# Query norms by transposes and accumulating squares early in a group, in place of products with ones at its end

## The chip, the cores and the metric

The kernel runs on one core of a Trainium2 chip. A core has a matrix engine (TensorE, PE in the profile; PEld is its loading of weights), a vector engine (VectorE, DVE), an engine for activations (ScalarE, ACT), GpSimd (POOL), and queues for transfers, here issued by SyncE (SP). The engines run side by side, each works through its own queue in order, and they wait for each other by semaphores. The metric is the device time of one execution in microseconds. Before the change the median of three runs is 860.6 us (859.97 to 862.24).

## What is computed

One decoder layer on 256 tokens of width 2048: a gated DeltaNet branch and a cross-attention into 256 memory tokens read one input projection; their outputs are gated and go through one output projection. The change touches the end of the DeltaNet branch, where queries are normed and outputs are normed:

```python
q = l2_norm(q) * DN_HEAD_DIM ** -0.5       # per token and head
...
o = gated_delta_rule(q, k, v, g, beta)     # linear in q, in chunks
o = rms_norm(o, out_g)
...
y = jnp.concatenate([mix, xa], axis=-1) * jax.nn.silu(z)
x = x + jnp.einsum("bse,ed->bsd", y, w_out[i])
```

The output is linear in q, so the kernel doesn't norm q: it folds the sum of squares of a query into the epsilon of the output's norm (eq in the code), and needs that sum per token only when the output o of a head is scaled.

## The kernel before

**Tiling and stream.** All weights (273 loads of 128x1024) come one after the other in the order of the list PLAN; I count them from 0. For each load SP starts a transfer into a tile st (five buffers), ACT casts it to the high part of wt (L335, four buffers), DVE subtracts to get the low part (L339), and PE runs 12 or 16 matmuls with high and low parts into pa (keys and queries) or pb (values, gates z, output projection). In the output projection the moving operands are yhi and ylo.

**Side work.** Everything else is generators that PE's stream passes now and then (`step_side`): they give a plan of the time for each engine, and emit their instructions between two matmuls of the stream. `pe_soon` makes a generator wait until PE may take its next block, `until` and `bank` wait for a condition or a free bank of PSUM (tags "m" and "A" have two, "B" one). All of this happens while the program is built. After 45 us of the plan the instructions are put in order by the framework, so that the final order on each engine differs somewhat from the order of the code, and a change of one step moves others. On the chip the order of each engine is fixed.

**A group.** `delta(g)` works on group g of six: two pairs of query and key heads, four value heads. In turn: products pkq of keys and queries (km, kch, kcl); products pU with the inverse Y of the first chunk (u0s, u0, uh, ul); products across the chunks and the first block of pO; products with the second half of Y (u1) and across again (oq); then ACT squares the queries `KQ[p][:, 1]` of both pairs into q2, and PE runs the second pO block and four products pqs of q2 with a column of ones, which give the sums of squares per token. DVE then computes o[1] = pO + oq and eq from pqs; ACT squares o with accumulation (ojunk); DVE computes e = (mean square + eq); POOL raises it to -1/2 (the function `rsqrt`, e<-e,mhalf); DVE scales o by e and by the gates zs, eight times 128x128 a group.

**The outputs.** `split_y` takes the finished outputs by twos of pairs, transposes them on PE (eight transposes into pyT), and writes yhi (ACT) and ylo (DVE). GATHER_Y is the time that it is willing to wait until another generator wants PE, so that their blocks go together. The output projection holds at the first weight whose ylo isn't there.

**The convolution of values** (vc, of vs and taps vw) and of queries and keys (raw, acc) is also DVE work between the loads; inT and inXT belong to the inverse's substitution, pm to its products on PE.

Of the kernel before, what the change touches and what calls it, by code (L numbers as in the profile page):

```python
# [10 lines left out]
AF = mybir.ActivationFunctionType  # L11
ALU = mybir.AluOpType
# [9 lines left out]
NB = 2  # L22
C = 128
EPS = 1e-6
# [9 lines left out]
LOOK = 2  # L34
WARM = 8
GATHER = 0.5
GATHER_Y = 4.0
XPACE = 3.0
HOP = 0.25
PINNED = 45.0  # L40
# [32 lines left out]
def hybrid_kernel(ctx: ExitStack, tc: tile.TileContext, x, xT, memT, W, prm_d, cst_d, out):  # L73
# [32 lines left out]
    def width(ap):  # L106
        n = 1
        for d in ap.shape[1:]:
            n *= d
        return n  # L110
# [14 lines left out]
    ve, se = Engine(nc.vector, ve_cost), Engine(nc.scalar, se_cost)  # L125
# [19 lines left out]
    def S2(name, shape, dt=F32):  # L145
        return s2p.tile([128] + list(shape), dt, name=name, tag="s2")

    def SM(name, shape, bufs=3, dt=F32):
        n = 1
        for d in shape:  # L150
            n *= d
        if n > 128:
            return smp.tile([128] + list(shape), dt, name=name, tag="s1k", bufs=6)
        if n > 16:
            return smp.tile([128] + list(shape), dt, name=name, tag="s512", bufs=3)
        return smp.tile([128] + list(shape), dt, name=name, tag=name, bufs=bufs)

    PB = {"pa": 3, "m": 2, "A": 2, "B": 1}

# [4 lines left out]
    def PS(tag, name):  # L164
        idle[tag].remove(min(idle[tag]))
        pt = ps.tile([128, 512], F32, name=name, tag=tag, bufs=PB[tag])
        held[id(pt)] = (tag, pt)
        return pt

    def spare(tag, n=1):  # L170
        return sum(t <= now[0] for t in idle[tag]) >= n

    def give(pt, t):

        idle[held.pop(id(pt))[0]].append(t)

    def bank(tag, name):
        yield from until(lambda: spare(tag))
        return PS(tag, name)

    def banks(name):
        yield from until(lambda: spare("m", 2))
        return [PS("m", name) for _ in range(2)]
# [10 lines left out]
    def mm(o_, lhsT, rhs, start, stop):  # L194
        n = width(rhs)
        if rhs.dtype == F32:
            now[0] += {32: 0.015, 64: 0.038}.get(rhs.shape[0], max(0.19, 4 * n / 2400.0))
        else:
            now[0] += max(0.092, n / 2400.0 + 0.0137) + 0.01 * (n == 256)
        te.matmul(o_, lhsT, rhs, start=start, stop=stop)  # L200

    def tr(o_, i_):
        now[0] += 0.093
        te.transpose(o_, i_, ident)
# [25 lines left out]
    def until(cond):  # L230
        while not cond():
            yield POLL

    def pe_soon(gather=0.0):

        yield max(fin[0] - now[0], 0.0) + SLACK
        yield "pe", gather
# [9 lines left out]
    def calm(queued=CALM):  # L247

        while ve.end > now[0] + queued:
            yield ve.end - now[0] - queued  # L250
# [5 lines left out]
    ones = cst[:, K_ONE : K_ONE + 1]  # L256
# [606 lines left out]
    KQ = [None] * NPAIR  # L863
# [242 lines left out]
    def split_y():  # L1106
        for j0 in (12, 14, 0, 2, 4, 6, 8, 10):
            jj = (j0, j0 + 1)
            yield from until(lambda: all(yf[j] is not None for j in jj))
            yield from calm(0.8)  # L1110
            yield "pe", GATHER_Y
            pts = yield from banks("pyT")
# [45 lines left out]
    def v_done(g):  # L1158
# [13 lines left out]
        def done(r, pt):  # L1172
            def go():
# [41 lines left out]
                if r == 1:  # L1215
                    vss[g] = raw
                    yield from delta(g)
# [8 lines left out]
    def delta(g):  # L1226

        pp = (2 * g, 2 * g + 1)
# [24 lines left out]
            ve.tensor_tensor(out=kcl[:, i], in0=pkv[i][:, 0:4:2, :], in1=kch[:, i], op=ALU.subtract)  # L1253
            give(pks[i], ve.end)
        yield from pe_soon(GATHER)
        A = yield from bank("A", "pU")
        for w, i, h in heads:
            mm(A[:, w * C : (w + 1) * C], Y[pp[i]][:, 0, h, :], vs[0][:, w, :], start=True, stop=True)
        yield 0.2
        u0s, u0 = S2("u0s", [4, C]), S2("u0", [4, C])  # L1260
        ve.tensor_tensor(out=u0s, in0=A.rearrange("j (h e) -> j h e", h=4),
                         in1=ekd[:, h4].unsqueeze(2).to_broadcast([128, 4, C]), op=ALU.mult)
        se.copy(u0.rearrange("j h e -> j (h e)"), A)
        give(A, max(ve.end, se.end))
        yield
        uh, ul = S2("uh", [4 * C], F32R), S2("ul", [4 * C], F32R)
        u0f = u0s.rearrange("j h e -> j (h e)")
        se.copy(uh, u0f)
        for i, p in enumerate(pp):
            ve.tensor_tensor(out=aT[i], in0=km[:, i].unsqueeze(2).to_broadcast([128, NB, 2, C]), in1=dT[p], op=ALU.mult)  # L1270
        yield
        ve.tensor_tensor(out=ul, in0=u0f, in1=uh, op=ALU.subtract)
        yield from pe_soon(GATHER)
        yield from until(lambda: spare("A") and spare("B"))
        A, B = PS("A", "pU"), PS("B", "pO")
# [19 lines left out]
        A, B = PS("A", "pU"), PS("A", "pO")  # L1295
# [8 lines left out]
        for w in range(4):  # L1304
            se.activation(oq[:, w, :], B[:, w * C : (w + 1) * C], AF.Copy, scale=egc[:, 4 * g + w : 4 * g + w + 1])
        give(B, se.end)
        q2 = S2("q2", [2, 256])
        for i, p in enumerate(pp):
            se.activation(q2[:, i, :], KQ[p][:, 1, :], AF.Square)
        yield from pe_soon(GATHER)  # L1310
        yield from until(lambda: spare("B") and spare("m"))
        B, pq = PS("B", "pO"), PS("m", "pqs")
        for w, i, h in heads:
            mm(B[:, w * C : (w + 1) * C], aT[i][:, 1, h, :], u1[:, w, :], start=True, stop=True)
        for b in range(NB):
            for i in range(2):
                mm(pq[:, 2 * b + i : 2 * b + i + 1], q2[:, i, b * C : (b + 1) * C], ones, start=True, stop=True)
        yield 0.2
        ve.tensor_tensor(out=o[1], in0=B.rearrange("c (h e) -> c h e", h=4), in1=oq, op=ALU.add)
        give(B, ve.end)  # L1320

        eq, e4 = SM("eq", [4], 2), SM("e4", [3, NB, 4], 2)
        ve.tensor_scalar(out=eq, in0=pq[:, 0:4], scalar1=EPS, scalar2=EPS * 128, op0=ALU.add, op1=ALU.mult)
        give(pq, ve.end)
        ready.add(f"d{g}")
        yield
        for b in range(NB):
            for w in range(4):
                junk = SM("ojunk", [C])
# [161 lines left out]
```

## Time and profile before

| | before |
|---|---|
| median of 3 runs | 860.6 us |
| profiled execution | 861.81 us, its span 860.0 us |
| granted clock of TensorE | 1.0 |
| POOL busy | 46.5 us (5%) |
| e<-e,mhalf on POOL | 6 times, 1.64 to 6.49 us |
| pqs on PE | 48 records (each program product is two) |
| pyT of outputs o on PE | 48 records (one for each transpose) |

The page gives the busy time of each engine and, in the chain of waits, what released what on the way to the last instruction. Rows of the timeline read: start in us, length in us, engine, line, operation, written tile <- read tiles, shape, how many, and in brackets how long the engine stood idle before and what ended that. PE's records overlap, so the cost of a matmul is read from start to start, not from its length.

### The profile page before, as it was taken

The numbers are of one execution on the slowest core, as the hardware profiler recorded it, in microseconds if no ns is written. First come the engines' busy times: TensorE is split into PE (matmuls) and PEld (weight loads), VectorE is DVE, ScalarE is ACT, GpSimd is POOL, SyncE is SP. The second block draws the span as 40 slices with busy tenths as digits, with TensorE's granted clock in tenths as the row PEclk, the third lists the DMA queues.
The fourth block names the chain that finished last, engine by engine and source line by source line (L and its number), as shares of the span: only waits on it lengthen the run. The fifth ranks groups of instructions, "written<-read, shape, count | busy, mean of one in ns | idle before, by whom it ended". The sixth has DMA issues, their size and how long they took to land.

```text
span 860.0 us, 13169 instructions
## 1 busy us (share of the span) xinstructions
PE 851.7 (99%) x4789; PEld 711.4 (83%) x4789; DVE 619.3 (72%) x1080; ACT 538.7 (63%) x927; POOL 46.5 (5%) x45
## 2 busy tenths in 40 slices
PE   8999999999999999999999999999999999999998
PEld 5888888888888888888888888787888888888886
DVE  7778896658679974788889999568886665444442
ACT  7655654797744665895976666679875654333331
POOL 1000000000000000001100301100010000000000
PEclk9999999999999999999999999999999999999999
DMA  9865566448677886769867779676754547666650
GB/s 352 307 203 177 170 182 168 152 134 259 206 218 228 261 233 206 253 200 266 241 229 232 217 229 269 204 219 228 239 158 161 177 145 255 231 204 207 201 196 24
DMA packets 145289, 181.59 MB, mean 211 GB/s; under 512 B 24808, under 2 KB 115808, under 8 KB 145224
## 3 DMA queue, kind: packets, MB, share of 16 engines
q1 hardware_dynamic: 144792, 180.47, 66.4%
q8 instruction: 37, 0.61, 0.3%
q10 hardware_dynamic: 432, 0.28, 0.1%
q14 instruction: 28, 0.23, 0.1%
HBM read 167.58 MB, written 6.89 MB: 203 GB/s over the span
## 4 chain that ended last, share of the span: by engine, by line
PE 89%; DVE 3%; ACT 3%; DMA 2%; issue 1%; SPq 0%; ACTq 0%; DVEq 0%
PE pb L86 69%; PE pa L86 11%; PE pO L86 2%; PE pU L86 2%; DMA vc<-vs 1%; DVE wt L339 1%; PE pm L86 1%; DVE vc L103 1%; PE pkq L86 1%; PE pyT L86 1%; ACT dec L103 1%; DMA mst<-memT_d 1%; PE pqs L86 1%; DVE acc L103 1%; PE pkk L86 1%
## 5 line engine op out<-in xcount | busy, mean ns | idle before, releaser
L339 DVE TENSOR_TENSOR wt<-st,wt 128x1024 fp32r<-128x1024 f32 (+1 forms) x274 | 332.3, 1216 | 168.4 <-ACT wt L335 161.4
L335 ACT CAST wt<-st 128x1024 fp32r<-128x1024 f32 (+1 forms) x274 | 286.2, 1048 | 232.9 <-PE pb L86 191.9
L86 PE MATMUL pb<-wt,hkt 128*128 128x512 f32 x1536 | 362.3, 393 | 1.5 <-DVE wt L339 1.5
L86 PEld LDWEIGHTS pb<-wt,hkt 128*128 128x128 f32 x1536 | 284.6, 188 | 60.7 <-DVE wt L339 2.5
L86 PE MATMUL pb<-wt,yhi 128*128 128x512 f32 x512 | 158.2, 390 | 0.0
L86 PE MATMUL pa<-hkt,wt 128*128 128x512 f32 (+1 forms) x768 | 142.7, 341 | 0.4 <-DVE wt L339 0.3
L86 PEld LDWEIGHTS pa<-hkt,wt 128*128 128x128 f32 x768 | 117.8, 188 | 18.2 <-DVE wt L339 1.0
L86 PEld LDWEIGHTS pb<-wt,yhi 128*128 128x128 f32 x512 | 95.8, 188 | 19.6
L86 PE MATMUL pb<-wt,ylo 128*128 128x512 f32 x256 | 99.7, 389 | 0.0
L86 PE MATMUL pb<-wt,mkt 128*128 128x512 f32 x384 | 92.4, 401 | 1.2 <-DVE mkt L103 0.7
L86 PEld LDWEIGHTS pb<-wt,mkt 128*128 128x128 f32 x384 | 73.6, 193 | 18.9 <-ACT wt L335 1.6
L86 PEld LDWEIGHTS pb<-wt,ylo 128*128 128x128 f32 x256 | 48.1, 188 | 10.1
L103 ACT ACT_TABLE_LOAD x31 | 39.8, 1283 | 1.4 <-DVE acc L103 1.0
L103 DVE SCALAR_TENSOR_TENSOR acc<-raw,prm,acc 128x255 f32<-128x255 f32 (+2 forms) x72 | 34.2, 476 | 3.5 <-ACT acc L103 3.2
L103 DVE TENSOR_TENSOR inT<-inXT,inN 96x1 f32<-96x1 f32 (+22 forms) x92 | 29.2, 343 | 2.5 <-DMA inN<-dN 1.7
L103 DVE TENSOR_REDUCE inXT<-inT 96x1 f32<-96x1 f32 (+22 forms) x92 | 28.6, 338 | 0.7
L103 POOL TENSOR_TENSOR e<-e,mhalf 128x8 f32<-128x8 f32 x6 | 20.8, 3474 | 120.3 <-DVE e L103 120.3
L103 DVE TENSOR_TENSOR vc<-vc 128x512 f32<-128x512 f32 x36 | 24.5, 684 | 0.1
L103 POOL TENSOR_TENSOR srk<-skt,mhalf 128x4 f32<-128x4 f32 x6 | 7.1, 1176 | 224.7 <-DVE skt L103 224.7
L103 DVE SCALAR_TENSOR_TENSOR o<-o,e,zs 128x128 f32<-128x128 f32 x48 | 14.0, 344 | 7.0 <-POOL e L103 7.0
L103 DVE TENSOR_TENSOR vc<-vc,vw 128x512 f32<-128x512 f32 x24 | 16.4, 685 | 3.4 <-DMA vc<-vs 2.7
L103 ACT ACTIVATE ojunk<-o 128x128 f32<-128x128 f32 x48 | 14.4, 301 | 5.7 <-DVE o L103 3.7
(202 smaller groups left out, 692.9 us busy)
## 6 DMA issues: line engine op xcount, KB each, us to landing
st<-W_d SPq DMA_DIRECT2D x272, 512.0 KB
erow<-dgc SPq DMA_DIRECT2D x24, 256.0 KB
vw<-dtap SPq DMA_DIRECT2D x24, 256.0 KB
dN<-dec SPq DMA_DIRECT2D x12, 256.0 KB
n<-dN SPq DMA_DIRECT2D x12, 256.0 KB
vc<-vs SPq DMA_DIRECT2D x12, 224.0 KB
vc<-vc SPq DMA_DIRECT2D x12, 224.0 KB
xraw<-xT_d SPq DMA_DIRECT2D x8, 256.0 KB
```

Source lines behind the costliest of these rows:

```text
L86: return lambda *a, **k: pin(getattr(self.eng, op)(*a, **k))
L103: return pin(getattr(self.eng, op)(*a, **k))
L335: pin(se.eng.copy(hi[:, w] if parts > 1 else hi, st[:, w] if parts > 1 else src))
L339: pin(ve.eng.tensor_tensor(out=lo[:, w] if parts > 1 else lo, in0=st[:, w] if parts > 1 else src, in1=hi[:, w] if parts > 1 else hi, op=AL ...
```

## The change

GATHER_Y goes from 4.0 to 0.5. The sums of squares of the queries are computed earlier in the group and by other engines: behind the pU products PE transposes the four 128x128 blocks of queries (query and chunk of tokens) into a bank pqT, and ACT squares each with accumulation along the row, which gives q2, one column for each of the four blocks. The two squares of 128x256 and the four products with ones go. The wait for a bank "m" moves with them, from the step with the second pO to that with pU.

```diff
-GATHER_Y = 4.0
+GATHER_Y = 0.5
...
         yield from pe_soon(GATHER)
-        A = yield from bank("A", "pU")
+        yield from until(lambda: spare("A") and spare("m"))
+        A, pq = PS("A", "pU"), PS("m", "pqT")
         for w, i, h in heads:
             mm(A[:, w * C : (w + 1) * C], Y[pp[i]][:, 0, h, :], vs[0][:, w, :], start=True, stop=True)
+        for w in range(4):
+
+            tr(pq[:, w * C : (w + 1) * C], KQ[pp[w % 2]][:, 1, w // 2 * C : (w // 2 + 1) * C])
...
         se.copy(uh, u0f)
+        q2 = SM("q2", [4], 2)
+        for w in range(4):
+            junk = SM("ojunk", [C])
+            se.activation(junk, pq[:, w * C : (w + 1) * C], AF.Square, accum_out=q2[:, w : w + 1])
+        give(pq, se.end)
...
-        q2 = S2("q2", [2, 256])
-        for i, p in enumerate(pp):
-            se.activation(q2[:, i, :], KQ[p][:, 1, :], AF.Square)
         yield from pe_soon(GATHER)
-        yield from until(lambda: spare("B") and spare("m"))
-        B, pq = PS("B", "pO"), PS("m", "pqs")
+        yield from until(lambda: spare("B"))
+        B = PS("B", "pO")
         for w, i, h in heads:
             mm(B[:, w * C : (w + 1) * C], aT[i][:, 1, h, :], u1[:, w, :], start=True, stop=True)
-        for b in range(NB):
-            for i in range(2):
-                mm(pq[:, 2 * b + i : 2 * b + i + 1], q2[:, i, b * C : (b + 1) * C], ones, start=True, stop=True)
...
-        ve.tensor_scalar(out=eq, in0=pq[:, 0:4], scalar1=EPS, scalar2=EPS * 128, op0=ALU.add, op1=ALU.mult)
-        give(pq, ve.end)
+        ve.tensor_scalar(out=eq, in0=q2, scalar1=EPS, scalar2=EPS * 128, op0=ALU.add, op1=ALU.mult)
```

Since the framework puts the instructions in order, others move too. Three places matter below.

**Group 0, DVE, around load 134 (gates z).** Before, from o = pO + oq on; the two rows of wt are loads 134 and 135:

```order
L103 TENSOR_TENSOR o<-pO,oq 128x512
L103 TENSOR_TENSOR raw<-raw 128x256 [waits Activation_49]
L339 TENSOR_TENSOR wt<-st,wt 128x1024 [waits DMAHW0_49,PE_49]
L103 SCALAR_TENSOR_TENSOR acc<-raw,prm,acc 128x255 [waits Activation_49]
L103 SCALAR_TENSOR_TENSOR e_4173<-e_4173,eq 128x8 [waits Activation_49]
L339 TENSOR_TENSOR wt<-st,wt 128x1024 [waits DMAHW3_49,PE_49]
L103 SCALAR_TENSOR_TENSOR acc<-raw,prm,acc 128x254 [waits DVE_49]
L103 TENSOR_TENSOR vc<-vc 128x512 [waits DMAHW7_49,DMAHW6_49,DMAHW0_49]
L103 SCALAR_TENSOR_TENSOR acc<-raw,prm,acc 128x253 [waits DVE_49]
L103 TENSOR_TENSOR vc<-vc 128x512 [waits DMAHW2_49,DMAHW1_49,Pool_49]
L103 SCALAR_TENSOR_TENSOR o<-o,e_4173,zs 128x128 [waits Pool_49]
```

Now, from behind load 133 on; the row of wt at the end is load 134:

```order
L103 TENSOR_TENSOR vc<-vc 128x512 [waits DMAHW2_49,DMAHW1_49,DMAHW0_49]
L103 TENSOR_TENSOR raw<-raw 128x256 [waits Activation_49]
L103 TENSOR_TENSOR inT<-inXT,inN 96x1 [waits DMAHW6_49,DMAHW3_49,Pool_49]
L103 COPY inN<-inXT 96x16x16 [waits Pool_49]
L103 TENSOR_TENSOR vc<-vc 128x512 [waits DMAHW7_49,DMAHW6_49,DVE_49]
L103 SCALAR_TENSOR_TENSOR e_4167<-e_4167,eq 128x8 [waits Activation_49]
L103 TENSOR_REDUCE inXT<-inT 96x1 [waits DVE_49]
L103 SCALAR_TENSOR_TENSOR o<-o,e_4167,zs 128x128 [waits Pool_49]
L103 SCALAR_TENSOR_TENSOR acc<-raw,prm,acc 128x255 [waits Activation_49]
L103 SCALAR_TENSOR_TENSOR o<-o,e_4167,zs 128x128
L103 SCALAR_TENSOR_TENSOR acc<-raw,prm,acc 128x254 [waits DVE_49]
L339 TENSOR_TENSOR wt<-st,wt 128x1024 [waits DMAHW5_49,Activation_49]
```

Load 134 stood ahead of e; now it stands behind e, behind the wait for POOL, and behind two of the scalings of o. Three loads ahead of these rows the whole convolution of a value tile (twelve steps on vc, raw and acc) has moved from behind load 131 to ahead of it.

**Group 2, loads 175 and 176 (values).** DVE before, from load 175 to load 176:

```order
L339 TENSOR_TENSOR wt<-st,wt 128x1024 [waits DMAHW0_49,Activation_49]
L103 TENSOR_TENSOR vc<-vs,vw 128x512
L103 TENSOR_TENSOR vc<-vc,vw 128x512
L103 TENSOR_TENSOR vc<-vc 128x512 [waits DVE_49]
L103 TENSOR_TENSOR vc<-vc 128x512 [waits DMAHW4_49,DMAHW5_49,DVE_49,Pool_49]
L339 TENSOR_TENSOR wt<-st,wt 128x1024 [waits DMAHW6_49,PE_49,Activation_49]
```

DVE now, from the third step behind load 175 to load 176:

```order
L103 TENSOR_TENSOR vc<-vc 128x512 [waits DMAHW1_49,DMAHW2_49,DMAHW0_49,DVE_49]
L103 TENSOR_TENSOR vc<-vc 128x512 [waits DVE_49]
L103 TENSOR_TENSOR o<-pO,oq 128x512 [waits PE_49,Activation_49]
L103 TENSOR_TENSOR vc<-vc 128x512 [waits DMAHW6_49,DMAHW7_49,DVE_49,Pool_49]
L103 SCALAR_TENSOR_TENSOR e_5562<-e_5562,eq 128x8 [waits Activation_49]
L103 SCALAR_TENSOR_TENSOR o<-o,e_5562,zs 128x128 [waits DMAHW3_49,Pool_49]
L103 SCALAR_TENSOR_TENSOR o<-o,e_5562,zs 128x128
L103 SCALAR_TENSOR_TENSOR o<-o,e_5562,zs 128x128 [waits DVE_49]
L339 TENSOR_TENSOR wt<-st,wt 128x1024 [waits DMAHW5_49,Activation_49]
```

On PE the last matmuls of load 175 and what follows them, before:

```order
L86 MATMUL pb_5498<-wt,hkt 128x512 x3
L86 MATMUL pb_5472<-wt,hkt 128x512 x3
L86 MATMUL pb_5498<-wt,hkt 128x512 x3
L86 MATMUL pm<-Am,XN 32x32 [waits DMAHW6_49,Activation_49]
L86 MATMUL pm<-Am,XN 32x32 [waits DMAHW0_49]
```

and now:

```order
L86 MATMUL pb_5439<-wt,hkt 128x512 x3
L86 MATMUL pb_5455<-wt,hkt 128x512 x3
L86 MATMUL pO<-u_5498,aT 128x128 [waits PE_49,Activation_49]
L86 MATMUL pO<-u_5498,aT 128x128 x3
L86 MATMUL pm<-Am,XN 32x32 [waits DMAHW6_49,Activation_49]
```

The second pO block of group 2 has moved to between load 175 and the inverse's block on Am; before it stood eight loads earlier. On DVE the sum o, e, and three scalings, which wait for POOL, have come in ahead of load 176. On ACT the cast of load 176 now stands behind the four squares of that o.

**Group 3, DVE, between loads 185 and 187 (values).** Before, from load 186 to load 187:

```order
L339 TENSOR_TENSOR wt<-st,wt 128x1024 [waits DMAHW2_49,PE_49]
L103 SCALAR_TENSOR_TENSOR acc<-raw,prm,acc 128x255 [waits Activation_49]
L103 TENSOR_TENSOR u0s<-pU,ekd 128x512 [waits PE_49]
L103 SCALAR_TENSOR_TENSOR acc<-raw,prm,acc 128x254 [waits DVE_49]
L103 TENSOR_TENSOR vc<-vc 128x512 [waits DMAHW5_49,DMAHW4_49,Pool_49]
L103 SCALAR_TENSOR_TENSOR acc<-raw,prm,acc 128x253 [waits DVE_49]
L103 TENSOR_TENSOR vc<-vs,vw 128x512
L103 TENSOR_TENSOR vc<-vc,vw 128x512
L103 TENSOR_TENSOR aT<-km,dec 128x512
L103 TENSOR_TENSOR vc<-vc 128x512 [waits DVE_49]
L103 TENSOR_TENSOR aT<-km,dec 128x512
L339 TENSOR_TENSOR wt<-st,wt 128x1024 [waits DMAHW3_49,Activation_49]
```

Now, the eleven steps from raw on, ahead of load 186:

```order
L103 TENSOR_TENSOR raw<-raw 128x256 [waits Activation_49]
L103 TENSOR_TENSOR vc<-vc 128x512 [waits DVE_49]
L103 SCALAR_TENSOR_TENSOR acc<-raw,prm,acc 128x255 [waits Activation_49]
L103 TENSOR_TENSOR vc<-vc 128x512 [waits DMAHW3_49,DMAHW4_49,DVE_49,Pool_49]
L103 SCALAR_TENSOR_TENSOR acc<-raw,prm,acc 128x254 [waits DVE_49]
L103 SCALAR_TENSOR_TENSOR acc<-raw,prm,acc 128x253 [waits DVE_49]
L103 TENSOR_TENSOR vc<-vs,vw 128x512
L103 TENSOR_TENSOR vc<-vc,vw 128x512 [waits DMAHW7_49,DMAHW6_49,DMAHW0_49]
L103 TENSOR_TENSOR km<-pkq,cst 128x256 [waits PE_49]
L103 TENSOR_TENSOR vc<-vc 128x512 [waits DVE_49]
L103 TENSOR_TENSOR km<-pkq,cst 128x256 [waits PE_49]
L339 TENSOR_TENSOR wt<-st,wt 128x1024 [waits DMAHW2_49,Activation_49]
```

Before, ten steps of the group and of the convolution stood between two weights. Now pkq and pU of this group come later, the steps on u0s and aT stand between other loads, and the most crowded stretch is this one ahead of load 186, with a vc step ahead of its first row.

At the end of the program the last outputs' transposes, which stood on PE ahead of load 222's first matmul, now stand behind its ninth.

## The prediction

> **What bounds the kernel now.** First the page: busy times, then the chain of waits.
>
> ```profile
> span 860.0 us, 13169 instructions
> ...
> PE 851.7 (99%) x4789; PEld 711.4 (83%) x4789; DVE 619.3 (72%) x1080; ACT 538.7 (63%) x927; POOL 46.5 (5%) x45
> ...
> PE 89%; DVE 3%; ACT 3%; DMA 2%; issue 1%; SPq 0%; ACTq 0%; DVEq 0%
> ```
>
> PE is busy for 99% of the span and carries 89% of the chain. So an edit pays only in two ways: it takes instructions out of PE's row of matmuls, or it changes how often PE stands still. The view of PE's waits prices the second (total, times, longest):
>
> ```profile
> PE pb L86 <- DVE wt L339: 2.0, 4, 1.1
> ```
>
> Once it runs, PE waits for nothing but weights whose low part DVE has not yet written, 2.0 us in four waits. Two of the four fall at 580.96 and 594.09 in PE's timeline (start, length, count):
>
> ```profile
> 411.60 9.79 PE L86 MATMUL pb<-wt,hkt 128*128 128x512 f32 x42
> ...
> 577.64 2.88 PE L86 MATMUL pb<-wt,hkt 128*128 128x512 f32 x12
> 580.96 0.73 PE L86 MATMUL pb<-wt,hkt 128*128 128x512 f32 x2 [0.44 <-DVE wt L339]
> ...
> 590.83 2.20 PE L86 MATMUL pb<-wt,hkt 128*128 128x512 f32 x9
> 594.09 3.52 PE L86 MATMUL pb<-wt,hkt 128*128 128x512 f32 x14 [1.06 <-DVE wt L339]
> ```
>
> The first row gives the pace: 42 matmuls, the last 0.39 us long, so (9.79-0.39)/41 = 0.229 us from start to start. By it 580.96 is 0.6 us late (577.64 + 12 x 0.229 = 580.39) and 594.09 is 1.2 us late: 1.8 us together.
>
> **PE's work.** The end of group 5 shows what a product with ones and a transpose cost between two weight matmuls:
>
> ```profile
> 695.84 0.39 PE L86 MATMUL pb<-wt,ylo 128*128 128x512 f32 x1
> 696.07 1.05 PE L86 MATMUL pO<-u,aT 128*128 128x128 f32 x8
> 696.96 0.95 PE L86 MATMUL pqs<-cst,q 128*128 128x1 f32 x8
> 697.77 0.72 PE L86 MATMUL pb<-wt,yhi 128*128 128x512 f32 x2
> ...
> 701.77 0.39 PE L86 MATMUL pb<-wt,ylo 128*128 128x512 f32 x1
> 702.00 1.03 PE L86 MATMUL pyT<-cst,o 128*128 128x128 f32 x8
> 702.79 0.71 PE L86 MATMUL pb<-wt,yhi 128*128 128x512 f32 x2
> ```
>
> The 16 records of pO and pqs add 697.77-695.84-0.229 = 1.70 us, 0.106 each; a group's four products are eight records and take 0.85 us. The eight transposes add 702.79-701.77-0.229 = 0.79 us, 0.099 each, so four new ones take 0.40 us. Saved: 0.45 us a group, **2.7 us** for six. I take the transposes of KQ at the price of pyT, since shape and type are the same. At their recorded length (about 0.27 us, were they not overlapped) four would cost 1.1 us; that end is a rival below.
>
> GATHER_Y only lets the outputs' transposes go sooner and less often together with other blocks. In the rows above pO with pqs in one block and pyT in a block of its own cost the same per record (0.106 and 0.099): I take nothing for it.
>
> **ACT.** Two squares of 256 columns go, four accumulating ones come:
>
> ```profile
> 409.71 0.74 ACT L103 ACTIVATE q<-kq 128x256 f32<-128x256 f32 x2
> ...
> 697.95 0.31 ACT L103 ACTIVATE ojunk<-o 128x128 f32<-128x128 f32 x1 [1.98 <-DVE o L103]
> 698.16 0.19 ACT L103 ACTIVATION_READ_ACCUMULATOR ojunk<-o 128x1 f32 x1
> 698.25 0.29 ACT L103 ACTIVATE ojunk<-o 128x128 f32<-128x128 f32 x1
> ```
>
> One square and its read take 698.25-697.95 = 0.30 us, so 1.2 us come for 0.74: +0.5 us a group on an engine that is 63% busy. They now stand behind the copy uh, and behind them wait casts of weights and later copies of the group. The group of casts on the page shows the cover:
>
> ```profile
> L335 ACT CAST wt<-st 128x1024 fp32r<-128x1024 f32 (+1 forms) x274 | 286.2, 1048 | 232.9 <-PE pb L86 191.9
> ```
>
> ACT idles 232.9 us ahead of casts, 191.9 of them until PE gives a buffer back: casts start as soon as a buffer is free, which is long before PE needs it filled. Were that cover gone, 1.2 us a group would be late where it matters, 7 us at most; I take nothing. The same row prices what moves on SP's queue (around group 0 the shifts of values are issued a load earlier, ahead of the weights of load 132): casts wait for PE, not for the transfers, so a load that lands a microsecond later is hidden, and I take nothing there either.
>
> The wait for a bank of "m" moves from the step with pO to the step with pU. It is a condition while the program is built, and no instruction waits longer for it as such; what it does is push pU back in the order, in group 3 from load 183 to load 185. What follows from that is priced in the groups below.
>
> **What the order moves, group 0.** New on DVE is that the low part of load 134 stands behind e, POOL's power and two scalings. The rows of before that price it, group 5's tail first (DVE and POOL):
>
> ```profile
> 697.16 0.69 DVE L103 TENSOR_TENSOR o<-pO,oq 128x512 f32<-128x512 f32 x1
> ...
> 699.26 0.17 DVE L103 SCALAR_TENSOR_TENSOR e<-e,eq 128x8 f32<-128x8 f32 x1 [1.15 <-ACT ojunk L103]
> 701.24 0.88 DVE L103 SCALAR_TENSOR_TENSOR o<-o,e,zs 128x128 f32<-128x128 f32 x3 [1.82 <-POOL e L103]
> 702.04 1.22 DVE L339 TENSOR_TENSOR wt<-st,wt 128x1024 fp32r<-128x1024 f32 x1
> ...
> 699.57 1.64 POOL L103 TENSOR_TENSOR e<-e,mhalf 128x8 f32<-128x8 f32 x1 [41.52 <-DVE e L103]
> ```
>
> ```profile
> 416.64 0.42 DVE L103 TENSOR_TENSOR raw<-raw 128x256 f32<-128x256 f32 x1 [0.49 <-ACT raw L103]
> ...
> 420.03 0.48 DVE L103 SCALAR_TENSOR_TENSOR acc<-raw,prm,acc 128x254 f32<-128x254 f32 x1
> 420.43 0.69 DVE L103 TENSOR_TENSOR vc<-vc 128x512 f32<-128x512 f32 x1
> 421.03 0.48 DVE L103 SCALAR_TENSOR_TENSOR acc<-raw,prm,acc 128x253 f32<-128x253 f32 x1
> ```
>
> raw waited for ACT until 416.64, and I leave it there. Behind it now come two small steps on inT and inN and a vc ahead of e: 0.6 for the vc (421.03-420.43), at most 0.42 for raw, and 0.3 each for the small ones, an estimate near raw's. That is 1.6 us, so e starts at 418.2. From e to the first scaling group 5 took 701.24-699.26 = 1.98 us; two scalings (0.3 each) and two acc (0.40, from 420.03 to 420.43) make 1.4; the low part takes 1.22. Load 134 is ready at 422.8. PE wants it 38 matmuls after 411.60, at 420.3, and 0.45 us earlier by the work saved. PE stands for 422.8-419.9 = **2.9 us**. Below: if raw comes 0.7 us sooner, 2.2. Above: if the value convolution, now ahead of load 131, starts no earlier than before, everything is some 1.2 us later, and POOL may be slow: 5.0.
>
> **Group 2.** The second pO block now stands right behind load 175's matmuls, and load 176 is behind the whole tail on DVE (o, e, POOL, three scalings) and its cast behind the four squares of o on ACT. It is group 5's tail word for word: the low part started 702.04-696.07 = 5.97 us after pO, ready at 7.2. PE meanwhile has pO (0.89, from 696.07 to 696.96) and the inverse's block:
>
> ```profile
> 552.72 0.26 PE L86 MATMUL pm<-Am,XN 32*32 32x32 f32 x8
> ...
> 554.69 1.19 PE L86 MATMUL pb<-wt,hkt 128*128 128x512 f32 x4
> ...
> 552.43 1.23 DVE L339 TENSOR_TENSOR wt<-st,wt 128x1024 fp32r<-128x1024 f32 x1 [3.94 <-ACT wt L335]
> ```
>
> That block takes 1.97 us and a start of 0.1; before, load 176 was ready (552.43 + 1.23) a microsecond ahead of its use at 554.69. Now PE wants it 3.0 us after pO begins: it stands for 7.2-3.0 = **4.2 us**. Nothing below 3.5 follows from these rows unless group 2's pO comes earlier than its place in the order; the upper end is POOL's:
>
> ```profile
> 534.67 4.83 POOL L103 TENSOR_TENSOR e<-e,mhalf 128x8 f32<-128x8 f32 x1 [13.13 <-DVE e L103]
> ...
> 535.58 0.68 DVE L103 TENSOR_TENSOR vc<-vs,vw 128x512 f32<-128x512 f32 x1
> ...
> 419.06 2.56 POOL L103 TENSOR_TENSOR e<-e,mhalf 128x8 f32<-128x8 f32 x1 [11.76 <-DVE e L103]
> ```
>
> The same eight columns took 4.83 and 2.56 us while DVE worked on vc, and 1.64 where DVE stood still (699.57). At both new places DVE stands still behind the power, so I take 1.64; with the longer ones 3.2 and 0.9 us are added.
> [...]
>
> **Group 3.** The two waits at 580.96 and 594.09 go: the blocks of six and ten steps ahead of loads 183 and 187 are broken up, and the most crowded gap now lies ahead of load 186 (twelve steps; with 0.6 for a vc and 0.4 for the others 6.0 us). With two low parts of 1.22 that makes 8.4 us from the cast of load 185; a buffer is four loads old, 4 x 12 x 0.229 = 11 us, when PE comes to it, and km, pU and the new transposes lengthen that. Load 186 still lands some 2 to 3 us early. **-1.8 us**; if a like wait forms there, nothing.
>
> **The end.** The last outputs' transposes move back by nine matmuls, to three before their first use. In before (PE, ACT):
>
> ```profile
> 716.50 1.03 PE L86 MATMUL pyT<-cst,o 128*128 128x128 f32 x8
> ...
> 717.65 1.26 ACT L103 ACTIVATE yhi<-pyT,prm 128x512 fp32r<-128x512 f32 x2
> ```
>
> From their start to the first yhi are 1.15 + 0.63 = 1.8 us; PE has 0.79 of them and 3 x 0.229 = 0.7: **+0.3 us**, between 0 and 0.6.
>
> **Sum.** -2.7 + 2.9 + 4.2 - 1.8 + 0.3 = +2.9 us: a span of 862.9, and with 1.8 us around it 864.7 for an execution like the profiled one (861.8). That one lies 1.2 us above the median of the three runs, 860.6, so I forecast **863.4**. A measurement here can tell about 0.3% from no change, 2.6 us: below 858.0 or above 863.2.
>
> **Rivals.**
> - Neither wait forms (0.12): DVE reaches the weights earlier than I think. Only work, group 3 and the end count: 856.4. For it: of all waits in before none is behind POOL's power. Against: the order puts the weights there.
> - One of the two forms (0.20): 859.2 with group 0's alone, 860.6 with group 2's.
> - POOL's power is long at both places (0.08), as in 534.67: 863.4 + 3.2 + 0.9 = 867.5, slower. It decides from about 1.6 us on.
> - PE falls back to half pace after standing 4.2 us (0.04). At the start it ran so:
>
> ```profile
> 1.21 3.59 PE L86 MATMUL warm<-warm 128*128 128x512 bf16 x8 [1.21 <-DVE warm L103]
> 8.67 4.63 PE L86 MATMUL pb<-wt,mkt 128*128 128x512 f32 x10 [0.27 <-DVE wt L339]
> ```
>
>   0.46 us a matmul for 4.6 us after the last pause, against 0.229 later: ten matmuls, 2.3 us, 865.7. Against: no pause in before is longer than 1.2 us once it runs, so no row shows a fall.
>   [...]
> - The transposes don't overlap (0.04): six groups pay 1.1 for 0.85 us, +1.5 in place of -2.7, 867.6. The pyT rows speak against it.
>
> **Chances.** My forecast has 0.52; spread by 1.3 us either way it lies a little more often above 863.2 than below, 0.28 to 0.24. With the rivals: slower 0.44, same 0.44 (one wait alone falls here), faster 0.12. The range leaves out the case without waits and the far ends of the slow ones: 858.4 to 866.8.
>
> **What would show it.** Right: PE with 4765 records; two waits of pb for wt of about 3 and 4 us, at some 420 and 555, each ending with a wt that follows o scalings after POOL's e; none at 580 and 592; POOL's e near 1.6 us there. Wrong: PE's wait for wt under 3 us in all, or a wait at places not named.

## The result, and the profile after

The changed kernel takes 869.3 us (867.9 to 871.4, four runs) beside 861.4 us before: the ratio is 1.0096, its 95% interval 1.0078 to 1.0114. It is slower, as forecast, but by some 8 us where 2.9 were worked out, and 869.3 lies above the range's end of 866.8. The profiled execution took 867.9 us against 861.8, so 6.1 us of the loss can be looked up in it. The page of the kernel after:

```profile
span 866.1 us, 13173 instructions
...
PE 852.8 (98%) x4765; PEld 711.3 (82%) x4765; DVE 619.6 (72%) x1080; ACT 541.1 (62%) x963; POOL 40.3 (5%) x45
...
PE 85%; issue 8%; ACT 2%; DMA 2%; DVE 1%; POOL 1%; ACTq 0%; SPq 0%; DVEq 0%; POOLq 0%
```

PE has 24 records less, as expected (4765), and is yet busy 1.1 us longer. Work that went but left PE busier means that some of its matmuls took longer. PE's waits in the kernel after:

```profile
PE pb L86 <- DVE wt L339: 3.2, 4, 2.4
PE pO L86 <- ACT u L103: 2.6, 1, 2.6
...
PE pm L86 <- issue: 1.0, 1, 1.0
```

There is one long wait for a weight, not two, and a new one for ACT's copy u. The long wait for a weight is group 2's. In the timeline after (PE, then DVE and POOL):

```profile
553.13 1.05 PE L86 MATMUL pO<-u,aT 128*128 128x128 f32 x8
557.28 0.73 PE L86 MATMUL pb<-wt,hkt 128*128 128x512 f32 x2 [0.26 <-ACT wt L335]
560.38 0.80 PE L86 MATMUL pb<-wt,hkt 128*128 128x512 f32 x1 [2.36 <-DVE wt L339]
...
565.84 2.93 PE L86 MATMUL pb<-wt,hkt 128*128 128x512 f32 x6
568.56 1.73 PE L86 MATMUL pa<-hkt,wt 128*128 128x512 f32 x7
...
554.29 0.69 DVE L103 TENSOR_TENSOR o<-pO,oq 128x512 f32<-128x512 f32 x1 [8.00 <-PE pO L86]
...
558.31 0.87 DVE L103 SCALAR_TENSOR_TENSOR o<-o,e,zs 128x128 f32<-128x128 f32 x3 [1.82 <-POOL e L103]
559.11 1.22 DVE L339 TENSOR_TENSOR wt<-st,wt 128x1024 fp32r<-128x1024 f32 x1
...
556.64 1.64 POOL L103 TENSOR_TENSOR e<-e,mhalf 128x8 f32<-128x8 f32 x1 [18.53 <-DVE e L103]
```

From pO to the low part of load 176 are 559.11-553.13 = 5.98 us; 5.97 was forecast. PE's waits there are 1.0 (in the inverse's block, for its own issue), 0.3 and 2.4 us. But behind the wait six matmuls take 2.93 us, about 0.46 from start to start ((2.93-0.63)/5, the last being 0.63 long) where 0.229 is the pace. The view by windows shows why (window, busy time of PE, PEld, DVE, ACT, POOL, granted clock, share of DMA, GB/s):

```profile
552.00:556.00 4.00, 3.01 (x81) 2.57 (x81) 1.29 (x2) 1.77 (x9) 0.00 (x0) 1.00 0.92 370
556.00:560.00 4.00, 1.76 (x94) 1.21 (x87) 1.85 (x5) 3.90 (x10) 2.10 (x2) 0.86 0.03 10
560.00:564.00 4.00, 3.62 (x23) 2.32 (x25) 2.77 (x7) 1.78 (x4) 0.52 (x1) 0.50 0.43 136
564.00:568.00 4.00, 4.00 (x39) 3.50 (x38) 1.23 (x1) 3.14 (x5) 0.00 (x0) 0.50 0.87 243
568.00:572.00 4.00, 4.00 (x46) 3.27 (x47) 2.45 (x2) 1.84 (x5) 0.00 (x0) 0.86 1.00 301
```

The clock is 0.5 for (0.14 + 0.5 + 0.5 + 0.14) x 4 / 0.5 = 10.2 us, from about 558.9 to 569.1. Some 8.7 us of that lie behind the end of the wait (560.4). If PE had work in all of them, half would be lost: 4.3 us at most. The work itself gives a little less. From 560.38 to 568.56, 8.18 us, PE runs ten matmuls of 128x512 into pb and a block of 48 products of 64x64 into pm; in a later run, e4, the same work at a clock of 1.00 takes 565.94-561.33 = 4.61 us. That is 3.6 us lost, and with 0.3 for the 0.6 us of half pace behind it **3.9 us**.

The other wait is group 0's (ACT, SP, PE, DVE):

```profile
407.84 1.04 ACT L335 CAST wt<-st 128x1024 fp32r<-128x1024 f32 x1 [2.76 <-DMA st<-W_d]
...
409.20 0.56 ACT L103 COPY u<-pU 128x512 f32<-128x512 f32 x1
...
396.52 4.46 SPq L86 DMA_DIRECT2D vc<-vs  x5
...
401.67 0.39 SPq L86 DMA_DIRECT2D st<-W_d  x1
...
404.77 2.46 PE L86 MATMUL pb<-wt,hkt 128*128 128x512 f32 x10
409.82 1.16 PE L86 MATMUL pO<-u,aT 128*128 128x128 f32 x8 [2.60 <-ACT u L103]
...
423.71 0.50 PE L86 MATMUL pb<-wt,hkt 128*128 128x512 f32 x1 [0.26 <-DVE wt L339]
...
422.44 1.22 DVE L339 TENSOR_TENSOR wt<-st,wt 128x1024 fp32r<-128x1024 f32 x1
```

ACT stands 2.76 us ahead of a cast, for a load that SP issued at 401.67, behind the five shifts of values. The copy u is in ACT's row behind that cast, and PE's pO waits for u. The same place in before (PE, ACT):

```profile
404.53 4.25 PE L86 MATMUL pb<-wt,hkt 128*128 128x512 f32 x18
408.86 1.16 PE L86 MATMUL pO<-u,aT 128*128 128x128 f32 x8
...
408.24 0.56 ACT L103 COPY u<-pU 128x512 f32<-128x512 f32 x1
```

So two things meet in this wait. The copy u is finished at 409.76 where it was finished at 408.80, 1.0 us later. And pO stands behind ten matmuls of pb where it stood behind eighteen, so that PE comes to it at 407.2 and not at some 408.8, 1.6 us sooner. Without the 2.76 us ahead of the cast u would be finished at 407.0 (an estimate from these rows), and pO would not wait.

Load 134, where 2.9 us were forecast, costs 0.3. Its low part is ready at 423.66, 0.9 us later than forecast, but PE, which stood for u, comes to it at 423.45, 3.5 us later than forecast, 2.6 of them the stand for u.

By these rows the loss in the profiled execution is -2.7 (PE's work) + 2.6 + 0.3 (group 0) + 3.7 (group 2) + 3.9 (the clock) - 1.8 (group 3: no wait at 580 or 592 any more) = +6.0 us, beside the 6.1 measured.

### The profile page after: what moved, and what is told of

Its sections match the earlier page's. It is cut to its first block, busy times and chain, and to the rows that moved or that the text cites. A ratio compares the mean times of both kernels' runs of the same rounds, so it can differ in the third digit from the quotient of the medians.

```text
span 866.1 us, 13173 instructions
## 1 busy us (share of the span) xinstructions
PE 852.8 (98%) x4765; PEld 711.3 (82%) x4765; DVE 619.6 (72%) x1080; ACT 541.1 (62%) x963; POOL 40.3 (5%) x45
## 4 chain that ended last, share of the span: by engine, by line
PE 85%; issue 8%; ACT 2%; DMA 2%; DVE 1%; POOL 1%; ACTq 0%; SPq 0%; DVEq 0%; POOLq 0%
PE pb L86 67%; PE pa L86 10%; PE pO L86 2%; PE pU L86 1%; PE pm L86 1%; PE pkq L86 1%; PE pyT L86 1%; DVE wt L339 1%; ACT L103 1%; DMA st<-W_d 1%; DMA mst<-memT_d 1%; ACT dec L103 1%; DMA erow<-dgc 0%; PE pab L86 0%; POOL e L103 0%
## 5 line engine op out<-in xcount | busy, mean ns | idle before, releaser
L103 POOL TENSOR_TENSOR e<-e,mhalf 128x8 f32<-128x8 f32 x6 | 14.8, 2474 | 131.8 <-DVE e L103 111.0
L103 ACT ACTIVATE dec<-erow,gcc 128x128 f32<-128x128 f32 x48 | 16.4, 395 | 2.8 <-DMA erow<-dgc 2.8
L103 ACT ACTIVATE dec<-erow,ngc 128x128 f32<-128x128 f32 x48 | 16.1, 393 | 2.7 <-DMA erow<-dgc 2.7
```

The lines of the kernel that those rows point to most:

```text
L103: return pin(getattr(self.eng, op)(*a, **k))
```

## The experiments

Two theories stood after this. **A**: the norms' part moves two places into a wait, and group 2's stretch of little work also drops the clock; the late load makes group 0's wait. **B**: the loss lies elsewhere: in the shorter gather, or in a clock that falls by itself, and group 0's wait in DVE's row around load 134, as the prediction had it. Ratios are to the kernel before, run on the same chip beside each kernel, with their 95% intervals.

**e1, e2: the two parts apart.**

```diff
 e1, in the changed kernel
-GATHER_Y = 0.5
+GATHER_Y = 4.0
 e2, in the kernel before
-GATHER_Y = 4.0
+GATHER_Y = 0.5
```

> The change with GATHER_Y left at 4.0. Its order is that of the changed kernel on every engine up to about load 186. If the loss comes from the norms' part (group 0's wait at 410, group 2's wait at 560 and the half pace behind it), it is still there: 868 to 871 us against 861.4 before, the granted clock under 1.0. If the shorter gather of the outputs' transposes causes it, 857 to 861 us and no half clock.

> The kernel before with GATHER_Y 0.5 and nothing else. If the loss comes from the norms' part: 860 to 863 us, clock 1.0. If from the gather: 866 us or more.

e1: 868.5 us, 1.0093 (1.0078 to 1.0108), the clock at 0.990 to 0.994 in its runs. e2: 861.5 us, 1.0006 (0.9993 to 1.0018). The whole loss comes with the norms; the gather does nothing that can be measured.
e2's profiled execution has something that the expectation didn't allow, a short fall of the clock. PE waits there 1.2 us for its own issue inside the inverse's block of 32x32 products, and then:

```profile
552.00:556.00 4.00, 2.83 (x149) 2.24 (x147) 1.22 (x1) 2.61 (x3) 0.00 (x0) 1.00 0.57 197
556.00:560.00 4.00, 4.00 (x17) 2.70 (x11) 0.00 (x0) 3.77 (x7) 0.00 (x0) 0.57 0.29 97
```

0.57 over 4 us are 3.4 us at half clock, some 1.7 us lost. So the clock can fall at this place without any long wait, here for a third of the time. How often it does isn't known, since one execution was profiled.

**e3: group 2 without its wait.**

```diff
-        return tc.keep_in_program_order(ins) if PINNED is None or now[0] < PINNED else ins
+        return tc.keep_in_program_order(ins) if PINNED is None or now[0] < PINNED or 535 < now[0] < 565 else ins
```

> The changed kernel, with the instructions that are planned between 535 and 565 us kept in the order of the code. DVE's row between loads 175 and 176 then holds no e and no scaling of group 2; all up to there is as in the changed kernel, group 0's wait too. If group 2's wait of 3.9 us also causes the half pace (8.5 us of work at half clock, 4.3 us lost), both go: 8 us, 861 us, clock 1.0 throughout. If the half pace comes by itself, only 3.9 us go: 865 us with a clock of 0.994. If the waits reappear elsewhere: 868 us or more.

859.4 us, 0.9987 (0.9972 to 1.0002): from 0.96% above before to 0.13% below, 9.4 us, a little more than the 8 expected. The profiled execution's clock is 1.0 throughout. Its DVE rows in group 2:

```profile
548.27 0.69 DVE L103 TENSOR_TENSOR o<-pO,oq 128x512 f32<-128x512 f32 x1 [2.24 <-PE pO L86]
552.46 1.23 DVE L339 TENSOR_TENSOR wt<-st,wt 128x1024 fp32r<-128x1024 f32 x1 [3.49 <-ACT wt L335]
...
554.20 0.16 DVE L103 SCALAR_TENSOR_TENSOR e<-e,eq 128x8 f32<-128x8 f32 x1
```

The weight now stands between o and e, and no longer behind POOL; pO itself comes some six microseconds sooner than in the changed kernel. Group 0's wait is still there (2.2 us for u).

**e4: the wait kept, the stretch of little work filled.**

```diff
         give(B, ve.end)
+        if g == 2:
+            F = PS("B", "fill")
+            for n in range(8):
+                nc.tensor.matmul(F, warm[:, 0:128], warm, start=True, stop=True)
+            give(F, ve.end)
```

> The changed kernel with eight matmuls of zeros (as in the warm-up, results unused) on PE in group 2, behind the second pO block, so that PE works for 1.7 us in the middle of the stretch in which it waits for load 176. The wait for load 176 stays where it was, so that PE's own work ends no sooner. If the stretch of little work drops the clock, the half pace goes and the wait stays: 869.3 - 4.3 = 865 us, clock 1.0. If the clock drops for another reason: 869 to 871 us, clock 0.994 or less.

865.5 us, 1.0056 (1.0039 to 1.0074), against 1.0096: 0.40%, 3.4 us less, by adding work. PE in group 2, and two of its windows:

```profile
554.09 1.05 PE L86 MATMUL pO<-u,aT 128*128 128x128 f32 x8
555.99 1.89 PE L1327 MATMUL fill<-warm 128*128 128x512 bf16 x8 [0.68 <-DVE o L103]
...
561.33 1.65 PE L86 MATMUL pb<-wt,hkt 128*128 128x512 f32 x6 [0.92 <-DVE wt L339]
...
565.94 2.05 PE L86 MATMUL pa<-hkt,wt 128*128 128x256 f32 x11
```

```profile
556.00:560.00 4.00, 4.00 (x152) 2.75 (x152) 1.44 (x5) 3.87 (x12) 2.10 (x2) 1.00 0.18 60
560.00:564.00 4.00, 3.08 (x13) 1.72 (x11) 3.88 (x9) 3.72 (x8) 0.52 (x1) 1.00 0.34 88
```

From pO to the matmul that waited for the low part are 561.33-554.09 = 7.24 us, and 560.38-553.13 = 7.25 in the changed kernel: the path over DVE and POOL is the same to the hundredth. Behind the wait the clock differs, 1.00 for 0.50. This separates the two prices: the half pace is worth 3.4 us by the medians' ratios (1.3 to 5.6 by their intervals), and 3.9 by the rows. The rest of the 9.4 us that e3 takes away is more than the 3.7 us of waits in the rows; the intervals allow the difference, and whether e3's order gains elsewhere too isn't known.

**e5, e8: group 0's wait.** Both start from e3.

```diff
 e5
-            sd.dma_start(dst[n : 112 + n], src[r][0:112])
-            sd.dma_start(dst[112 + n : 128], src[r][112 : 128 - n])
+            q = nc.scalar if g == 1 and n == 1 else sd
+            q.dma_start(dst[n : 112 + n], src[r][0:112])
+            q.dma_start(dst[112 + n : 128], src[r][112 : 128 - n])
             if r:
-                sd.dma_start(dst[0:n], src[0][128 - n : 128])
+                q.dma_start(dst[0:n], src[0][128 - n : 128])
 e8
-        return tc.keep_in_program_order(ins) if PINNED is None or now[0] < PINNED or 535 < now[0] < 565 else ins
+        return tc.keep_in_program_order(ins) if PINNED is None or now[0] < PINNED or 405 < now[0] < 425 or 535 < now[0] < 565 else ins
```

> The kernel of e3, and the five shifts of values (vc<-vs, first shift of value group 1) issued by ACT's queue instead of SP's, so that the load of weights 132 no longer stands behind them on SP. If group 0's wait (2.2 to 2.9 us before pO, for ACT's copy u) comes from load 132 landing late and holding ACT's queue, it goes: e3's 859.4 - 3 = 856.5 us. If it comes from DVE's row around load 134 (e, POOL, scalings), the wait moves to load 134's first matmul and the time stays at 859 to 860 us.

> The kernel of e3, and instructions planned between 405 and 425 us also in the order of the code: on DVE load 134 stands ahead of group 0's e again, on SP load 132 still behind the shifts. If the late load 132 is the cause, the wait of pO for u stays: 859 to 860 us. If DVE's row around load 134 is the cause, the wait goes: 856.5 us.

e8: 859.8 us, 0.9988 (0.9972 to 1.0003), no gain on e3. Load 134 is not ahead of e in it, as the expectation had it, but it is ahead of the scalings and their wait for POOL (its low part starts at 422.07, e at 420.55, the first scaling at 424.94). The wait is where it was:

```profile
405.85 2.46 PE L86 MATMUL pb<-wt,hkt 128*128 128x512 f32 x10
410.66 1.65 PE L86 MATMUL pO<-u,aT 128*128 128x128 f32 x6 [2.35 <-ACT u L103]
```

So DVE's row around load 134 isn't the cause of pO's wait. e5: 858.1 us, 0.9966 (0.9952 to 0.9981), 2.9 us under the kernel before: **a version that beats both**. Its rows (PE, ACT, DVE):

```profile
405.95 1.05 PE L86 MATMUL pO<-u,aT 128*128 128x128 f32 x8
...
410.12 2.14 PE L86 MATMUL pb<-wt,hkt 128*128 128x512 f32 x8 [1.03 <-DVE wt L339]
...
404.14 1.04 ACT L335 CAST wt<-st 128x1024 fp32r<-128x1024 f32 x1
405.08 0.59 ACT L103 COPY u<-pU 128x512 f32<-128x512 f32 x1
...
408.24 0.68 DVE L103 TENSOR_TENSOR vc<-vc,vw 128x512 f32<-128x512 f32 x1
408.85 1.22 DVE L339 TENSOR_TENSOR wt<-st,wt 128x1024 fp32r<-128x1024 f32 x1
```

No cast waits for a load, u is there in time, and pO doesn't wait, though it comes behind four matmuls of pb and not ten. Against e3 only about half of the expected 3 us arrives, 1.3 us by the medians and 1.8 by the ratios, hardly clear of the intervals: behind the wait that went the next one stands, 1.0 us for a weight whose low part is behind the whole value convolution in DVE's row.

**e6, e7: the shifts later in the plan.** Also from e3; the step that issues the first shift of group 1's values is put off.

```diff
+                if g == 1:
+                    yield 2.0
                 shift(a, val, r, 1)
```

(3.0 in e7.)

> The kernel of e3, and the value convolution of group 1 begins its shifts 2 us later in the plan. On SP the load of weights 132 then stands ahead of the shifts, as before the change; much behind it is in another order. If the late load is the cause of group 0's wait: no wait of pO for u near 410, 856 to 858 us unless another place opens a wait. If it isn't: the wait is still there.

> As e6 with 3 us: the loads up to 133 stand ahead of the shifts. Late load the cause: no wait of pO for u, 856 to 858 us; the most crowded stretch on DVE is one of thirteen steps ahead of load 195 (8 us by the steps' lengths), which may open a wait of 1 to 2 us. Otherwise the wait near 410 stays.

Misses, both. e6: 866.1 us, 1.0055 (1.0036 to 1.0073); e7: 859.8 us, 0.9990 (0.9972 to 1.0007). No cast stands for a load near 405 in e7, yet pO still waits 1.7 us for u: PE's row comes to pO at about 404.4 there, and ACT to u at 405.6, behind a row of decays, squares and a cast without a pause since 398.97, where it had waited 1.95 us for another transfer (erow). So the late load is one way in which u comes late, not the only one; the edit moves pO as well, and can't single out a cause. e6 has a new wait of 2.3 us for a cast, and the clocks of its runs are 0.990 to 0.996, beside 0.995 to 1.0 in e7's. How much of its 6 us over e7 these two account for isn't shown.

**e9: group 0 mended alone; e10: e5 with the long gather.**

```diff
 e9: the edit of e5 in the changed kernel, without that of e3
 e10, in e5
-GATHER_Y = 0.5
+GATHER_Y = 4.0
```

> The changed kernel with the five shifts issued by ACT's queue, and group 2 as the change has it. If the two places add up, group 0's part of the gain is what e5 gained on e3 (1.3 us) and group 2's wait and half pace stay: 869.3 - 1.3 = 868 us, clock 0.994 or less. If the half pace hangs on group 0 too (by the moment at which PE comes to group 2), the clock differs: 864 us or less.

> The kernel of e5 with GATHER_Y back at 4.0. Both blocks cost PE the same; e2 found no difference. 857 to 859.5 us, the same as e5 within 1.5 us. If the shorter gather is worth something in the changed order (the last outputs' transposes stand nine matmuls later with it), up to 0.5 us less; if the order behind load 186 opens a wait, 860 us or more.

e9: 866.5 us, 1.0069 (1.0042 to 1.0096), 0.27% or 2.3 us under the changed kernel's ratio, with pO's wait at 0.2 us and 4.2 us of waits for weights where the changed kernel has 3.2. The expectation was 1.3 us; the intervals allow both, and no gain as well. The clock is 0.994 in the profiled execution, as in the changed kernel's, and PE's longest wait for a weight is 2.4 us, as there, so that group 2's loss doesn't seem to hang on group 0. e10: 858.6 us, 0.9975 (0.9963 to 0.9987), the same as e5 within the intervals: the gather is worth nothing in this order either.

## Why the prediction was right in its sign and wrong in its size

- **PE's work: right.** The rows after show the transposes where a weight matmul stands on each side:

```profile
439.69 1.98 PE L86 MATMUL pb<-wt,hkt 128*128 128x512 f32 x8
441.51 1.05 PE L86 MATMUL pU<-vc,Y 128*128 128x128 f32 x8
442.40 0.60 PE L86 MATMUL pqT<-cst,kq 128*128 128x128 f32 x4
442.75 0.48 PE L86 MATMUL pb<-wt,hkt 128*128 128x512 f32 x1
...
709.59 0.39 PE L86 MATMUL pb<-wt,ylo 128*128 128x512 f32 x1
709.82 1.05 PE L86 MATMUL pO<-u,aT 128*128 128x128 f32 x8
710.62 0.71 PE L86 MATMUL pb<-wt,yhi 128*128 128x512 f32 x2
```

  pU and pqT add 442.75 - (439.69 + 7 x 0.229) - 0.229 = 1.23 us; a block of eight products alone adds 710.62-709.59-0.229 = 0.80. So the four transposes cost 0.43, forecast 0.40, and the rival in which they don't overlap (1.1) is out. pO with pqs had added 1.70, so the products were worth 0.90 (0.85 forecast). 0.47 a group, 2.8 us; 2.7 were taken.
- **GATHER_Y: right**, nothing (e2, e10). The last outputs' transposes, +0.3, stayed within a few tenths: the wait that ends the chain there, of PE for ylo, is 0.4 us on its load queue.
- **Group 2's wait: right** in place, cause and, nearly, size: 3.7 us for 4.2, with POOL at 1.64 as taken; the rival with a slow POOL is out. Most of the difference are the two matmuls at 557.28 (2 x 0.229 us): they need only the high part of load 176, and the forecast didn't let them run ahead of its low part. A microsecond of the 3.7 was inside the inverse's block, which PE itself issued late; the rows of before had shown no such gap.
- **Group 3: right**, both waits went.
- **Group 0: the size right, the cause wrong.** 2.9 us were forecast for load 134 behind POOL; 2.6 came as pO's wait for u, a wait at a place not named, and 0.3 at load 134. That the sum fits is luck as far as the runs show, and no support for the forecast's path: PE's stand for u came first, and PE came late to load 134 by it. What load 134 would cost with u in time isn't shown, since in e5 and e9, where u is in time, its low part stands ahead of the wait for POOL. The step that failed is the one on SP's queue: "casts wait for PE, not for the transfers, so a load that lands a microsecond later is hidden". In before, load 132 was issued at some 395, ahead of the shifts; after the change at 401.67, behind them. That is over six microseconds, not one, and all of ACT's row behind the cast waited, the copy u with it. And the forecast had no term for pO's earlier place on PE: at its old place, at some 408.8, it would have waited 1.0 us for u and not 2.6. e8 shows that DVE's row has no part in this, e5 that the wait goes when the load is early.
- **The clock: the step that broke the range.** "PE falls back to half pace after standing 4.2 us" had a chance of 0.04 and a price of 2.3 us, and no place in the sum. It happened in the profiled execution, and the clocks of the changed kernel's four runs (0.988 to 0.994, beside 0.995 to 1.0 in the runs of before) suggest it for the other three; it cost 3.9 us by the rows, 3.4 us by e4. Two things were wrong. The chance: that no row of before shows a fall was taken as evidence against it, but before had no stretch of that kind, and the forecast itself put a 4.2 us stand there. So the 0.04 was an estimate for which the rows gave no ground. In the trace it came without one long stand: the longest is 2.4 us. The price: it was read from ten matmuls at the start, 4.6 us at half pace, while here the clock was half for 10.2 us. The block of 64x64 products behind the wait ran in that time (561.1 to 565.9); what part it had in the length was not tested.
- The forecast plus the measured half pace, 2.9 + 3.4 to 3.9 us, is 6.3 to 6.8 us beside 6.1 in the profiled execution and 7.9 in the medians. What remains in the medians may in part be a longer time at half clock: the run of 871.4 us has a clock of 0.988, about twice the loss of the others. Where its other falls were isn't known, as only one execution was profiled, and not all of such a figure need be a loss: the profiled execution of e8 has 0.993, some 12 us at half by its span of 859.4 us (an estimate), of which the fall at 410 has 3.4, and took 861.2 us where two runs of e8 at 1.0 took 859.5 and 860.0. Nor does the figure count all: in before ten matmuls from 8.67 us on take 0.46 us each, twice the later 0.229, and it says 1.00 there.

## What to carry to other kernels

An edit that takes work from the engine that bounds the kernel is worth that work only if the order around it holds; here 2.8 us were saved and two places where the order moved, with the fall of the clock behind one of them, cost almost four times as much, and mending them gave the saving back. In an order that a framework makes, compare the transfers' queue as well as the engines: a load that slips behind a handful of small transfers stops every later instruction of the engine that waits for it, here for 2.8 us. And price a forecast wait of PE twice, once as time standing, once as the time at half clock that can follow it (group 2's: 3.7 us, and 3.4 to 3.9).

## What the runs showed of the hardware

- **The clock fell behind a gap of 1.2 us (e2) as well as behind a wait of 2.4 us (after).** e2 had no wait for another engine there but a gap of 1.2 us in a block of 32x32 products, and got 3.4 us at half clock. A wait of 2.35 us in e8 (410.66) was followed by a fall, one of 2.2 us at the same place in e3 wasn't:

```profile
410.00:414.00 4.00, 3.34 (x12) 3.05 (x13) 3.83 (x7) 3.27 (x11) 0.00 (x0) 0.59 1.03 227
```

  (e8; 0.59 are 3.3 us at half.) In the 4 us around the wait PE was busy for 1.65 us in e8 (408 to 412) and 1.77 in e3 (406 to 410). In after it was busy for 1.90 us from 555.5 to the fall at 558.9, 1.17 of them with products of 32x32. In after's record of the clock the time at half is 10.240 us, and the times at full ahead of it and behind it are 546.132 and 296.960 us: 3, 160 and 87 times 3.413 us. The falls of e2 and e8 have about that length (3.44 and 3.36 us by their windows). What decides whether the clock falls isn't shown by these runs.
- **Work for nothing can pay.** Eight matmuls of zeros in group 2's wait made the kernel 3.4 us faster (e4): the clock was 1.00 from 552 to 568, and 0.50 from 560 to 568 without them.
- **POOL's power took 1.64 us at both new places**, where DVE stood still, and up to 5.21 us elsewhere in the same execution, as the three rows of before had it (4.83, 2.56 and 1.64 us). Whether DVE's work makes it long, and what in it, wasn't tried.
- PE waited 0.8 to 1.2 us "for issue" inside the block of 32x32 products of group 2 in the changed kernel, e2 and e3, and not in the profiled execution of before. What causes that stays open.
